# Dense expert weights built in steps of eight tokens instead of four

## The chip, the cores and the metric

The kernel runs on one core of a Trainium2 chip. The metric is the device time of one execution in microseconds; the kernel before took 1877.42 us (median of three runs, 1877.06 to 1878.47). A profile of one execution comes with it. Engines are called by the profile's names: PE (TensorE matmul; PEld is its weight load), DVE (VectorE), ACT (ScalarE), POOL (GpSimd) and SP (SyncE, which issues most DMAs).

## The reference

The reference is one layer of a hybrid block on 512 tokens plus 16 meta tokens, 1024 features wide: a gated linear recurrence and a latent attention are mixed, and a mixture of 16,384 tiny experts (PEER) follows. Only the experts touch the change:

```python
q = (xt @ w_q).reshape(BLOCK, PEER_HEADS, PEER_QDIM)
s1 = jnp.einsum('chd,nd->chn', q[..., :half], keys1)
s2 = jnp.einsum('chd,nd->chn', q[..., half:], keys2)
...                                   # the 16 best (expert index idx, score ts) of each of 8 heads
g = jax.nn.softmax(ts, axis=-1)
act = jax.nn.gelu(jnp.einsum('chkd,cd->chk', u[idx], xt))
coef = g * act
return jnp.einsum('chk,chkd->cd', coef, v[idx])
```

So each token chooses 8 x 16 = 128 experts with one weight each.

## The kernel before

The tokens are four chunks of 128. For chunk 0 the rows of u and v are fetched by index. For the other three the kernel multiplies with both whole tables, in 128 blocks of 128 experts, and needs the softmax weights in dense form: an array [expert in block, block, token] that is zero wherever the token did not choose the expert. `scatter` (L843) makes that array for one chunk and writes it to DRAM (`gd`), from where the later loop loads it again (`gt`).

For one token, `scatter` forms two one-hot matrices with the 128 choices on the partitions: `hot`, which marks the expert's place in its block, and `hb`, which marks its block; `wj` is `hb` times the choice's weight. The product of `hot` and `wj` on PE, [expert in block, block], is the token's dense weight. Per step of four tokens:

- DVE compares for `hb` (L868, 512 columns, bf16; the four tokens are the innermost index) and for `hot` (L870, 512 columns, f32).
- ACT scales three of the four tokens' columns of `hb` into `wj` (L875), DVE the fourth (L877). Each reads every fourth bf16 element.
- PE does four 128 x 128 f32 products into one PSUM bank, side by side (L878). The trace shows each product as two matmuls.
- ACT copies the bank to `stg` (L879). `stg` is [block, 32 tokens] per partition, so a token's 128 values, which lie side by side in PSUM, go to places 128 bytes apart in SBUF.

After eight steps (32 tokens) SP writes `stg`, which has one buffer, to `gd` (L881). Four such pieces make a chunk, 96 steps the three chunks. `hb`, `hot` and `wj` have two buffers of four tokens each. The banks come from `mm2`, a ring of three (L453).

The three `scatter` generators are interleaved with two other streams by the share of each that is done: `choose` (L757), which finds the best pairs of the next chunk on DVE, and `first_ahead`, which computes the first expert product (u times x, then gelu) ahead of the main loop: nine, ten and twelve blocks beside the three chunks. Such a block is 24 PE matmuls of 128 x 384 (L181 to L183, tile `a`); its weights `ut_w` are split into two float32r parts, one by ACT (L155), one by DVE (L156), and its result goes through ACT's gelu (L820). A scheduler decides in which order the instructions stand on each engine; only the later loop fixes DVE's order (L976).

After the third chunk come the last two first products and then the main loop (`dense`, L958), which alternates a block of the first product with one of the second (tile `y`). Its operands `vh` and `vl` are in pool `vp`, opened before the scatter phase. The first `y` needs `gt`, and so the last `gd` transfer.

Of the kernel before, what the change touches and what calls it, by code (L numbers as in the profile page):

```python
# [21 lines left out]
NK = 8            # 128-row pieces of D_MODEL  # L22
NM = 16           # meta tokens
# [4 lines left out]
NH = 16           # attention heads  # L28
SCALE = 96.0 ** -0.5
PH = 8            # PEER heads  # L30
TOPK = 16
NS = PH * TOPK    # chosen experts of a token
NCAND = 50        # pairs (a, b) of ranks with (a + 1) * (b + 1) <= 16
NEG = -3.0e38
BIG = 1.0e30
# The pair of rank k (from 0) has (a + 1) * (b + 1) <= k + 1: blocks (a0, na, b0, nb) of pairs, by the
# group of four ranks that they can first have.
# [5 lines left out]
CO = (3, 0, 2, 1)    # chunks of queries of a pair of heads: the two sizes of the probabilities in turn  # L43
NJ = 128          # blocks of 128 experts
LAG = 41          # blocks that the first product runs ahead of the second
TS = 32           # tokens of a piece of the dense weights
JG = 4            # blocks of a load of the dense weights
# How the experts of a chunk are computed. Chunk 0: rows of both tables fetched by index.
# Chunks 1 to 3: products with both whole tables, times the dense softmax weights.
NDC = 3  # L50
ORD = (mybir.EngineType.DVE,)
SCA = 3           # tokens of four that ScalarE scales
LT = 2            # blocks of the first product between the two phases
GE = 6            # steps by which the fetches of rows end early
GA = ((0, 2), (2, 5))          # gate tiles that are computed between those of the recurrent branch
# [3 lines left out]
DT = NDC * P      # tokens of the dense chunks  # L59

# columns of the packed per-feature vectors
# [7 lines left out]
class in_order:  # L69
    """Keeps the instructions of the given engines that are traced within in the order of the program."""  # L70
# [22 lines left out]
def now(gen):  # L93
    """Runs a generator through; what it returns."""
    while True:
        try:
            next(gen)
        except StopIteration as e:
            return e.value
# [7 lines left out]
def interleave(*gens):  # L107
    """Runs generators in step, by the share of each that is done."""
    items = [[g, n, 0] for g, n in gens if n]
    while items:  # L110
        it = min(items, key=lambda i: i[2] / i[1])
        try:
            it[2] += next(it[0]) or 1
        except StopIteration:
            items.remove(it)
# [3 lines left out]
def hybrid_block_kernel(ctx: ExitStack, tc, hT, x, win, wkr, vecs, wgate, wrnn, watt, wuq, wukv, wout,  # L119
# [38 lines left out]
    wn = [0, 0, None]         # pieces, more buffers of the parts and their pool  # L158

    def wload(src, n, name):  # L160
        """A weight tile of n columns: its two float32r parts, in pieces of 512 columns."""
# [28 lines left out]
    # K' of a head: 64 rows without position, then the rotated rows twice  # L190
# [12 lines left out]
    def bcast_rms(sq, pieces, dim, dst, name):  # L203
        """dst = sqrt(mean of squares + eps) of every token (column), on all partitions."""
        for t0, n in pieces:
            o = mm1(f"{name}_ss{t0}")
            for k, q in enumerate(sq):
                TE.matmul(o[:, :n], onesP, q[:, t0:t0 + n], start=k == 0, stop=k == len(sq) - 1)
            A.activation(dst[:, t0:t0 + n], o[:, :n], AF.Sqrt, bias=eps_t, scale=1.0 / dim)

    # The projections take h * g; their outcomes are scaled by the token's 1/rms.
# [6 lines left out]
    def proj_tile(wi, full, name, src=None, m=P, w=None):  # L218
        """One tile of w_in: PSUM pieces (first token, tokens, psum); full: with the meta tokens."""
# [22 lines left out]
    def two(tags, name):  # L242
        """Eight [P, T] pieces in the space of two tiles."""
# [56 lines left out]
    def latent_norms():  # L300
        """The rotated key rows of all buffers, the normed latent of keys and values, the queries' scales."""
# [17 lines left out]
    # 8 * log_sigmoid(lambda) = 8 * (min(l, 0) - log1p(exp(-|l|)));  # L319
    # log1p(z) = 2 * atanh(y), y = z / (2 + z) <= 1/3  # L320
# [11 lines left out]
    for d in (13, 11, 9, 7, 5, 3, 1):  # L332
# [8 lines left out]
          for k in range(NK)]                              # recurrent output  # L341
    def sig_tile(wi, name):
        """Sigmoid of a tile of w_in."""
# [10 lines left out]
    def out_rnn(m):  # L354
        """A tile of the recurrent branch's gated outcome."""
# [11 lines left out]
    for hb in range(NK // HB):  # L367
# [53 lines left out]
        # 1 - a^2 = -tanh(log a) * (1 + a^2)  # L421
# [39 lines left out]
    def fm_pieces(pl, name):  # L461
        """A feature-major operand: the two parts of each 128-feature piece."""
# [5 lines left out]
    # the meta tokens in one product: rows hi, hi, lo of the values by hi, lo, hi of the probabilities  # L468
# [8 lines left out]
    def att_pair(pr):  # L477
        """Keys and values of a pair of heads."""
# [19 lines left out]
        # values of the tokens of each chunk  # L498
# [9 lines left out]
    def att_query(pr, j, pair):  # L508
        """Queries of a head."""
# [9 lines left out]
    def att_scores(st):  # L519
# [7 lines left out]
        for (k0, n), sp in zip(pieces, sps):  # L527
            d0 = nk - P - k0         # the diagonal block
# [20 lines left out]
    def att_turn(st):  # L549
        """Probabilities with the keys on the partitions, in parts; those of both heads side by side."""  # L550
# [21 lines left out]
    def att_out(st):  # L572
        """[feature of the pair, query of each head]: a head's own half of the features counts."""
# [54 lines left out]
    xdp = pool(ctx, "xd", "right")  # L628
    mx_ = pool(mixx, "mix")
    # normed input of the experts, feature-major: the dense chunks, then chunk 0  # L630
# [32 lines left out]
    def dense_products(j, o, w=None):  # L663
        """x . u of expert block j for the dense chunks: [expert, token]."""
# [7 lines left out]
    def mixing():  # L672
        """Attention output, gated sum of the branches, residual, second norm."""
# [50 lines left out]
    def key_scores():  # L724
        """Scores of the expert keys, the 16 best of each half."""
# [31 lines left out]
    def choose(i, c):  # L757
        """The 16 best pairs of each head, their indices and softmax weights."""
# [64 lines left out]
    def first_dense(j, o, w=None):  # L823
        """gelu(x . u) of expert block j for the dense chunks: [expert, token]."""
# [18 lines left out]
    def scatter(gi, val, ef):  # L843
        """Dense [expert in block, block, token] weights of a chunk, to DRAM: one-hot products of each token."""
# [17 lines left out]
        for q in range(P // TS):  # L862
            stg = sp_.tile([P, NJ, TS], F32, tag="stg", bufs=1, name=f"stg{gi}_{q}")
            for t4 in range(0, TS, 4):
                o = mm2(f"sc{gi}_{q}_{t4}")
                t0 = q * TS + t4
                hb = sp_.tile([P, P, 4], BF16, tag="hb", bufs=2, name=f"hb{gi}_{t0}")
                V.tensor_tensor(hb, iota4, blk[:, t0:t0 + 4].unsqueeze(1).to_broadcast([P, P, 4]), op=OP.is_equal)  # L868
                hot = sp_.tile([P, 4, P], F32, tag="hot", bufs=2, name=f"hot{gi}_{t0}")
                V.tensor_tensor(hot, iota.unsqueeze(1).to_broadcast([P, 4, P]),  # L870
                                it[:, t0:t0 + 4].unsqueeze(2).to_broadcast([P, 4, P]), op=OP.is_equal)
                wj = sp_.tile([P, 4, P], F32, tag="wj", bufs=2, name=f"wj{gi}_{t0}")
                for u in range(4):
                    if u < SCA:
                        A.activation(wj[:, u, :], hb[:, :, u], AF.Copy, scale=gt_[:, t0 + u:t0 + u + 1])  # L875
                    else:
                        V.tensor_scalar(wj[:, u, :], hb[:, :, u], gt_[:, t0 + u:t0 + u + 1], None, op0=OP.mult)  # L877
                    TE.matmul(o[:, u * P:(u + 1) * P], hot[:, u, :], wj[:, u, :], start=True, stop=True)  # L878
                A.copy(stg[:, :, t4:t4 + 4].rearrange("p j t -> p t j"), o.rearrange("p (t j) -> p t j", t=4))  # L879
                yield  # L880
            nc.sync.dma_start(gd[gi, q], stg)  # L881
# [24 lines left out]
    def first_by_index(c):  # L906
        """coef = softmax weight * gelu(u[idx] . x) of the chosen experts."""
# [31 lines left out]
    def stage(j):  # L939
        """Operands of step j: the parts of u of block j + LAG, of v and of the coefficients of block j."""  # L940
# [61 lines left out]
def _consts():  # L1002
    """Constants that depend on the shapes alone."""
# [22 lines left out]
def _layout(i):  # L1026
# [7 lines left out]
    def tiles(w):                      # [K, N] -> [N / 128][128 of K][K / 128 * 128 of N]  # L1034
# [17 lines left out]
    uq = np.concatenate([uq, uq[..., 80:96], uq[..., 64:80]], -1)               # 3, p, h, 128  # L1052
    uq = uq.reshape(3, P, 8, 2, P).transpose(2, 1, 3, 0, 4).reshape(8, P, 768)
    kv = f["w_ukv"][0].reshape(2, P, 8, 2, 2, 64)                               # k, p, pair, j, (key, value), 64
# [28 lines left out]
```

## Time and profile before

| what | value |
|---|---|
| median of three runs | 1877.42 us |
| lowest, highest | 1877.06, 1878.47 us |
| span of the profiled execution | 1876.3 us |
| PE, DVE, ACT busy over the span | 97%, 78%, 52% |
| mean granted TensorE clock | 0.996 |

The span runs from the first to the last instruction of one profiled execution; the page gives no other time for it. The span lies 1.1 us under the median of the timed runs. The scatter phase, in which the change lies, is the stretch from 720 to 967 us. Busy shares over the whole span mix stages with different limits, so the stage's own rows are what counts.

### The profile page before, as it was taken

To read this page: it belongs to the slowest core of one execution; us is meant where nothing else is said; L and a number is where in the kernel's file an instruction comes from. 1 tells how busy PE (TensorE), PEld (TensorE's weight loads), DVE (VectorE), ACT (ScalarE), POOL (GpSimd) and SP (SyncE) were. 2 spreads that over 40 slices of the span, in tenths; PEclk is the share of its full clock that TensorE was granted. 3 is DMA by queue.
4 is the path that set the end of the run, shared out by engine and by line. 5 is a ranking of instruction groups with operands and counts; after the bars stand their busy time and mean duration, and the time that the engine had idled before them with its cause. 6 is when DMAs were issued, how large, how long until landed. Compare 5 with 4: busy or idle time off the path is not lost.

```text
span 1876.3 us, 28456 instructions
## 1 busy us (share of the span) xinstructions
PE 1821.0 (97%) x9731; PEld 1600.0 (85%) x9731; DVE 1470.3 (78%) x3280; ACT 981.4 (52%) x1915; POOL 356.4 (19%) x295
## 2 busy tenths in 40 slices
PE   8999999999999999999999999999999999999997
PEld 7888778877788888888899999998999999998886
DVE  7787677777546999898858788787887888887775
ACT  5778576766334337999963333333333333333343
POOL 0100000000100000000014344344444444443310
PEclk9999999999999999999999999999999999999999
DMA  5333212112733223454569999989998899988764
GB/s 162 92 101 104 74 54 66 62 55 85 241 113 129 85 85 130 144 194 158 189 225 348 321 318 340 326 300 322 324 334 313 304 331 321 343 309 280 266 223 152
DMA packets 181602, 390.34 MB, mean 208 GB/s; under 512 B 16593, under 2 KB 68305, under 8 KB 179921
## 3 DMA queue, kind: packets, MB, share of 16 engines
q1 hardware_dynamic: 141632, 245.97, 38.9%
q0 software_dynamic: 39536, 142.00, 21.8%
q8 instruction: 76, 1.25, 0.3%
q14 instruction: 70, 0.57, 0.1%
q10 hardware_dynamic: 288, 0.56, 0.1%
HBM read 353.44 MB, written 34.08 MB: 207 GB/s over the span
## 4 chain that ended last, share of the span: by engine, by line
PE 73%; ACT 10%; DMA 6%; DVE 6%; issue 3%; POOL 0%; DVEq 0%; ACTq 0%; SPq 0%; POOLq 0%
PE y L183 8%; PE y L182 8%; PE y L181 8%; PE a L183 7%; PE a L182 7%; PE a L181 7%; ACT stg L879 4%; PE q L181 2%; PE q L182 2%; PE wgr_ps L228 2%; PE q L183 2%; PE wga_ps L228 2%; PE wgn_ps L228 2%; PE sc L878 2%; ACT wj L875 2%
## 5 line engine op out<-in xcount | busy, mean ns | idle before, releaser
L183 PE MATMUL a<-xdh,ut_l 128*128 128x384 f32 x1024 | 346.3, 338 | 4.3 <-DVE ut_l L156 4.3
L181 PE MATMUL a<-xdh,ut_h 128*128 128x384 f32 x1024 | 348.1, 340 | 0.7 <-ACT act L820 0.5
L182 PE MATMUL a<-xdl,ut_h 128*128 128x384 f32 x1024 | 345.7, 338 | 0.3 <-DVE xdl L156 0.3
L155 ACT CAST ut_h<-ut_w 128x512 fp32r<-128x512 f32 x256 | 159.2, 622 | 330.3 <-DMA ut_w<-in_peer_uT_dram 281.7
L183 PE MATMUL y<-vh,cl 128*128 128x512 f32 x768 | 300.6, 391 | 0.0
L182 PE MATMUL y<-vl,ch 128*128 128x512 f32 x768 | 300.3, 391 | 0.0
L181 PE MATMUL y<-vh,ch 128*128 128x512 f32 x768 | 299.0, 389 | 1.3 <-ACT ch L155 1.3
L902 POOL DMA_INDIRECT u<-in_peer_u_dram,eidx x128 | 162.7, 1271 | 682.9 <-DMA gt<-gd 458.5
L902 POOL DMA_INDIRECT v<-in_peer_v_dram,eidx x128 | 175.2, 1369 | 262.6 <-DVE acc L922 233.6
L156 DVE TENSOR_TENSOR ut_l<-ut_w,ut_h 128x512 fp32r<-128x512 f32 x256 | 170.5, 686 | 52.2 <-ACT ut_h L155 51.7
L183 PEld LDWEIGHTS a<-xdh,ut_l 128*128 128x128 f32 x1024 | 193.0, 188 | 5.2 <-DVE ut_l L156 5.0
L181 PEld LDWEIGHTS a<-xdh,ut_h 128*128 128x128 f32 x1024 | 193.0, 188 | 4.7 <-ACT act L820 0.9
L182 PEld LDWEIGHTS a<-xdl,ut_h 128*128 128x128 f32 x1024 | 192.9, 188 | 3.9 <-DVE xdl L156 0.5
L156 DVE TENSOR_TENSOR vl<-vr,vh 128x1024 fp32r<-128x1024 f32 x128 | 157.6, 1232 | 40.6 <-ACT vh L155 40.4
L155 ACT CAST ch<-gt 128x384 fp32r<-128x384 f32 x128 | 65.7, 513 | 233.8 <-DVE gt L952 228.8
L922 DVE SCALAR_TENSOR_TENSOR acc<-v,coef,acc 128x1024 f32<-128x1024 f32 x128 | 164.1, 1282 | 11.3 <-DMA v<-in_peer_v_dram,eidx 9.2
L183 PEld LDWEIGHTS y<-vh,cl 128*128 128x128 f32 x768 | 144.1, 188 | 30.6 <-DVE cl L156 0.3
L181 PEld LDWEIGHTS y<-vh,ch 128*128 128x128 f32 x768 | 144.2, 188 | 30.0 <-ACT ch L155 2.1
L182 PEld LDWEIGHTS y<-vl,ch 128*128 128x128 f32 x768 | 144.1, 188 | 28.4
L913 DVE SCALAR_TENSOR_TENSOR jk<-u,xn 128x1024 bf16<-128x1024 f32 x128 | 156.5, 1222 | 14.7 <-DMA u<-in_peer_u_dram,eidx 12.2
L155 ACT CAST vh<-vr 128x1024 fp32r<-128x1024 f32 x128 | 133.7, 1045 | 31.7 <-PE y L183 26.9
L156 DVE TENSOR_TENSOR cl<-gt,ch 128x384 fp32r<-128x384 f32 x128 | 71.5, 559 | 80.9 <-ACT ch L155 80.9
(349 smaller groups left out, 3569.2 us busy)
## 6 DMA issues: line engine op xcount, KB each, us to landing
ut_w<-in_peer_uT_dram SPq DMA_DIRECT2D x256, 256.0 KB, 6.2
vr<-in_peer_v_dram SPq DMA_DIRECT2D x128, 512.0 KB, 6.4
gd<-stg SPq DMA_DIRECT2D x12, 2048.0 KB, 7.3
gt<-gd SPq DMA_DIRECT2D x96, 256.0 KB, 6.9
wq_w<-in_wq_dram SPq DMA_DIRECT2D x32, 256.0 KB, 2.7
wxr_w<-in_win_dram SPq DMA_DIRECT2D x16, 256.0 KB, 2.7
wgr_w<-in_win_dram SPq DMA_DIRECT2D x16, 256.0 KB, 2.8
wga_w<-in_win_dram SPq DMA_DIRECT2D x16, 256.0 KB, 2.6
```

The lines of the kernel that those rows point to most:

```text
L155: A.copy(dst_hi, src)
L156: V.tensor_sub(dst_lo, src, r32(dst_hi))
L181: TE.matmul(o, lh, rh, start=first, stop=False)
L182: TE.matmul(o, lh, rl, start=False, stop=False)
L183: TE.matmul(o, ll, rh, start=False, stop=last)
L228: TE.matmul(o[:m, :n], lhs, rhs[:, k, t0:t0 + n], start=k == 0 and i == 0, stop=k == NK - 1 and i == 2)
L875: A.activation(wj[:, u, :], hb[:, :, u], AF.Copy, scale=gt_[:, t0 + u:t0 + u + 1])
L878: TE.matmul(o[:, u * P:(u + 1) * P], hot[:, u, :], wj[:, u, :], start=True, stop=True)
L879: A.copy(stg[:, :, t4:t4 + 4].rearrange("p j t -> p t j"), o.rearrange("p (t j) -> p t j", t=4))
L902: G.indirect_dma_start(out=t, out_offset=None, in_=src, in_offset=bass.IndirectOffsetOnAxis(ap=eidx[:, s:s + 1], axis=0))
L913: V.scalar_tensor_tensor(jk, t, 1.0, xn2, op0=OP.mult, op1=OP.mult, accum_out=coef[:, s:s + 1])
L922: V.scalar_tensor_tensor(acc, t, coef[:, s:s + 1], acc, op0=OP.mult, op1=OP.add)
```

## The change

`scatter` works in 16 steps of eight tokens a chunk instead of 32 steps of four.

- `hb` and `hot` of eight tokens are each one DVE instruction of 1024 columns (`hb` as two groups of four tokens, so that the tokens are still the innermost index, by fours).
- All eight columns of `wj` are made on ACT. DVE's `tensor_scalar` is gone.
- `hot` and `wj` no longer have tiles of their own: they take the two buffers each of `vh` and `vl` in pool `vp`.
- The products of a step are recorded one step later, after the next step's one-hots (`products`). Their second bank comes from tag `s`, which has three buffers, besides the ring of three.
- The eviction walks block by block and the four tokens innermost: it writes runs of four values (16 bytes) into `stg` and reads PSUM at steps of 512 bytes.

```diff
-SCA = 3
+SG = 8
...
-                wj = sp_.tile([P, 4, P], F32, tag="wj", bufs=2, name=f"wj{gi}_{t0}")
-                for u in range(4):
-                    if u < SCA:
-                        A.activation(wj[:, u, :], hb[:, :, u], AF.Copy, scale=gt_[:, t0 + u:t0 + u + 1])
-                    else:
-                        V.tensor_scalar(wj[:, u, :], hb[:, :, u], gt_[:, t0 + u:t0 + u + 1], None, op0=OP.mult)
-                    TE.matmul(o[:, u * P:(u + 1) * P], hot[:, u, :], wj[:, u, :], start=True, stop=True)
-                A.copy(stg[:, :, t4:t4 + 4].rearrange("p j t -> p t j"), o.rearrange("p (t j) -> p t j", t=4))
-                yield
-            nc.sync.dma_start(gd[gi, q], stg)
+        def products(t0, hot, wj, stg):
+            q, t8 = divmod(t0, TS)
+            for h in range(0, SG, 4):
+                o = ps.tile([P, 512], F32, tag="s", bufs=3, name=f"sc{gi}_{t0 + h}") if h else mm2(f"sc{gi}_{t0}")
+                for u in range(4):
+                    TE.matmul(o[:, u * P:(u + 1) * P], hot[:, h + u, :], wj[:, h + u, :], start=True, stop=True)
+                A.copy(stg[:, :, t8 + h:t8 + h + 4], o.rearrange("p (t j) -> p j t", t=4))
+            if t8 + SG == TS:
+                nc.sync.dma_start(gd[gi, q], stg)
+        last = None
+        for t0 in range(0, P, SG):
...
+            hb = sp_.tile([P, SG // 4, P, 4], BF16, tag="hb", bufs=2, name=f"hb{gi}_{t0}")
+            V.tensor_tensor(hb, iota4.unsqueeze(1).to_broadcast([P, SG // 4, P, 4]),
+                            blk[:, t0:t0 + SG].rearrange("p (h t) -> p h t", t=4).unsqueeze(2)
+                            .to_broadcast([P, SG // 4, P, 4]), op=OP.is_equal)
+            hot = r32(vp.tile([P, D], F32R, tag="vh", bufs=2, name=f"hot{gi}_{t0}")).rearrange("p (t e) -> p t e", t=SG)
...
+            wj = r32(vp.tile([P, D], F32R, tag="vl", bufs=2, name=f"wj{gi}_{t0}")).rearrange("p (t e) -> p t e", t=SG)
+            for u in range(SG):
+                A.activation(wj[:, u, :], hb[:, u // 4, :, u % 4], AF.Copy, scale=gt_[:, t0 + u:t0 + u + 1])
+            yield
+            if last:
+                products(*last)
+            last = (t0, hot, wj, stg)
+            yield
+        products(*last)
```

Comments and docstrings went as well, so the line numbers shift: the products are L869, the eviction L870, `wj` L888.

What it does to the order on PE shows at the start of the first chunk. Here `a` is a block of the first product, `sc` a bank of the scatter products; before, they stand so:

```order
L182 MATMUL a_7763<-xdl,ut_h_7664 128x384
L878 MATMUL sc_0_0_7702<-wj_0_7707,hot_0_7705 128x128 x4
L183 MATMUL a_7763<-xdh,ut_l_7665 128x384
L878 MATMUL sc_0_4_7717<-wj_4_7722,hot_4_7720 128x128 x2
L181 MATMUL a_7763<-xdh,ut_h_7670 128x384
...
L878 MATMUL sc_0_4_7717<-wj_4_7722,hot_4_7720 128x128 x2
L878 MATMUL sc_0_8_7732<-wj_8_7737,hot_8_7735 128x128 x4
L181 MATMUL a_7763<-xdh,ut_h_7670 128x384
```

In the changed kernel the same place on PE reads:

```order
L183 MATMUL a_7744<-xdh,ut_l_7671 128x384
L869 MATMUL sc_0_7771<-wj_0_7706,hot_0_7704 128x128 x4
L869 MATMUL sc_4_7777<-wj_0_7706,hot_0_7704 128x128 x4
L869 MATMUL sc_8_7796<-wj_8_7719,hot_8_7717 128x128 x4
L869 MATMUL sc_12_7802<-wj_8_7719,hot_8_7717 128x128 x4
L181 MATMUL a_7853<-xdh,ut_h_7734 128x384
```

Products that stood singly or in twos and fours inside a block of the first product now stand, mostly eight or sixteen together, between two blocks.

The second place is ACT at the end of the third chunk, where `stg` is the last piece, `act` a gelu and `vh` a part of the main loop's first operands. Before:

```order
L875 ACTIVATE wj_124_10634<-hb_124_10630,gt_9596 128x128
L155 CAST ut_h_10709<-ut_w_10707 128x512
L820 ACTIVATE act_10612<-a_10587 128x384
L879 COPY stg_3_10437<-sc_3_24_10614 128x4x128
L879 COPY stg_3_10437<-sc_3_28_10629 128x4x128
L155 CAST ut_h_10715<-ut_w_10713 128x512
```

And in the changed kernel:

```order
L888 ACTIVATE wj_120_10371<-hb_120_10367,gt_9436 128x128 x4
L870 COPY stg_3_10204<-sc_112_10380 128x128x4
L870 COPY stg_3_10204<-sc_116_10386 128x128x4
L155 CAST ut_h_10469<-ut_w_10467 128x512
L870 COPY stg_3_10204<-sc_120_10392 128x128x4
L155 CAST vh_10523<-vr_10521 128x1024
L870 COPY stg_3_10204<-sc_124_10398 128x128x4
L155 CAST vh_10546<-vr_10544 128x1024
```

Four evictions instead of two follow the last `wj`, with two other casts between them; the first two casts for `vh` now stand here, since `hot` holds these buffers until then. On PE three whole blocks of the first product follow the last `sc` before the first `y`, in both kernels.

## Rows read from the trace of the kernel before

**Rows 1.** The page, chain that ended last: shares by engine.
```profile
PE 73%; ACT 10%; DMA 6%; DVE 6%; issue 3%; POOL 0%; DVEq 0%; ACTq 0%; SPq 0%; POOLq 0%
```

**Rows 2.** Windows: stretch, length, busy of each engine (instructions), clock, DMA share, GB/s.
```profile
720.00:967.00 247.00, 228.97 (x1501) 212.87 (x1501) 212.76 (x681) 229.81 (x490) 0.00 (x0) 1.00 0.47 166
967.00:1000.00 33.00, 32.17 (x168) 29.52 (x167) 20.21 (x32) 11.10 (x20) 12.05 (x10) 1.00 1.03 363
1000.00:1850.00 850.00, 848.24 (x4188) 758.67 (x4187) 680.42 (x908) 313.21 (x501) 325.89 (x246) 1.00 0.89 308
```

**Rows 3.** Groups, 720 to 967: busy us, mean ns | idle before, its releasers.
```profile
L878 PE MATMUL sc<-wj,hot 128*128 128x128 f32 x768 | 109.6, 285 | 17.8 <-ACT wj L875 12.1 <-DVE hot L870 1.8 <-DVE wj L877 1.3
L879 ACT COPY stg<-sc 128x512 f32<-128x512 f32 x96 | 101.6, 1111 | 4.0 <-DMA gd<-stg 3.0 <-PE sc L878 0.6
L875 ACT ACTIVATE wj<-hb,gt 128x128 f32<-128x128 bf16 x288 | 98.2, 412 | 5.7 <-DVE hb L868 5.2
L878 PEld LDWEIGHTS sc<-wj,hot 128*128 128x128 f32 x768 | 97.8, 191 | 33.6 <-ACT wj L875 31.2 <-ACT stg L879 1.5
L870 DVE TENSOR_TENSOR hot<-iota,it 128x512 f32<-128x512 f32 x96 | 65.7, 684 | 2.7 <-PE sc L878 2.1
...
L868 DVE TENSOR_TENSOR hb<-iota,blk 128x512 bf16<-128x512 bf16 x95 | 39.3, 418 | 14.6 <-ACT wj L875 13.2 <-ACT blk L856 1.4
L155 ACT CAST ut_h<-ut_w 128x512 fp32r<-128x512 f32 x61 | 38.2, 629 | 7.7 <-PE a L182 7.6
L877 DVE TENSOR_SCALAR wj<-hb,gt 128x128 f32<-128x128 bf16 x96 | 26.8, 279 | 0.3 <-ACT gt L860 0.3
L820 ACT ACTIVATE act<-a 128x384 f32<-128x384 f32 x30 | 15.1, 502 | 0.2
```

**Rows 4.** Timeline of ACT, 804 to 813: start, length, instructions merged.
```profile
803.88 1.61 ACT L875 ACTIVATE wj<-hb,gt 128x128 f32<-128x128 bf16 x5
...
806.00 2.94 ACT L879 COPY stg<-sc 128x512 f32<-128x512 f32 x3
808.71 0.65 ACT L155 CAST ut_h<-ut_w 128x512 fp32r<-128x512 f32 x1
```

**Rows 5.** Timeline of PE, 962 to 965.5.
```profile
962.90 0.33 PE L183 MATMUL a<-xdh,ut_l 128*128 128x384 f32 x1
963.08 1.95 PE L878 MATMUL sc<-wj,hot 128*128 128x128 f32 x16
964.78 0.42 PE L181 MATMUL a<-xdh,ut_h 128*128 128x384 f32 x1
```

**Rows 6.** Groups of ACT and DVE, other shapes: busy us, mean ns.
```profile
L747 ACT COPY scs<-sc 128x512 f32<-128x512 f32 x16 | 9.4, 588 | 0.9 <-PE sc L745 0.7
L418 ACT ACTIVATE aa<-rr,cl 128x528 f32<-128x528 f32 x8 | 5.9, 737 | 0.1
L426 ACT ACTIVATE rr<-rr 128x528 f32<-128x528 f32 x8 | 4.9, 640 | 0.0
L810 ACT ACTIVATE gate<-gate 128x128 f32<-128x128 f32 x4 | 1.2, 311 | 0.0
L803 DVE TENSOR_TENSOR work<-sf,cand_pos 128x1600 bf16<-128x1600 bf16 x3 | 3.0, 983 | 0.0
L913 DVE SCALAR_TENSOR_TENSOR jk<-u,xn 128x1024 bf16<-128x1024 f32 x128 | 156.5, 1222 | 14.7 <-DMA u<-in_peer_u_dram,eidx 12.2
```

**Rows 7.** Timelines of ACT, SP and PE at the end of the phase.
```profile
964.17 2.04 ACT L879 COPY stg<-sc 128x512 f32<-128x512 f32 x2
...
966.23 0.33 SPq L881 DMA_DIRECT2D gd<-stg  x1
...
978.63 0.45 PE L181 MATMUL y<-vh,ch 128*128 128x512 f32 x1
```

More of the change, by code (lines that the diff above doesn't have):

```diff
@@ L861, in scatter @@
         yield
[L862 to L871, printed above, removed]
-                wj = sp_.tile([P, 4, P], F32, tag="wj", bufs=2, name=f"wj{gi}_{t0}")
-                for u in range(4):
-                    if u < SCA:
-                        A.activation(wj[:, u, :], hb[:, :, u], AF.Copy, scale=gt_[:, t0 + u:t0 + u + 1])
-                    else:
-                        V.tensor_scalar(wj[:, u, :], hb[:, :, u], gt_[:, t0 + u:t0 + u + 1], None, op0=OP.mult)
-                    TE.matmul(o[:, u * P:(u + 1) * P], hot[:, u, :], wj[:, u, :], start=True, stop=True)
-                A.copy(stg[:, :, t4:t4 + 4].rearrange("p j t -> p t j"), o.rearrange("p (t j) -> p t j", t=4))
-                yield
-            nc.sync.dma_start(gd[gi, q], stg)
@@ new lines, in scatter @@
+        last = None
+        for t0 in range(0, P, SG):
+            if t0 % TS == 0:
+                stg = sp_.tile([P, NJ, TS], F32, tag="stg", bufs=1, name=f"stg{gi}_{t0 // TS}")
+            hb = sp_.tile([P, SG // 4, P, 4], BF16, tag="hb", bufs=2, name=f"hb{gi}_{t0}")
[3 more added lines that the diff above has]
+            hot = r32(vp.tile([P, D], F32R, tag="vh", bufs=2, name=f"hot{gi}_{t0}")).rearrange("p (t e) -> p t e", t=SG)
+            V.tensor_tensor(hot, iota.unsqueeze(1).to_broadcast([P, SG, P]),
+                            it[:, t0:t0 + SG].unsqueeze(2).to_broadcast([P, SG, P]), op=OP.is_equal)
+            wj = r32(vp.tile([P, D], F32R, tag="vl", bufs=2, name=f"wj{gi}_{t0}")).rearrange("p (t e) -> p t e", t=SG)
[6 more added lines that the diff above has]
+            yield
```

## The prediction

> **What bounds the kernel now.** The chain of waits, read first, is three quarters PE, with ACT second at 10% [rows 1]. That is a mean over stages, so the windows come next: before 1000 us and after it the kernel has different limits. From 1000 to 1850 us PE is busy 848.2 of 850 us [rows 2]; that stage is PE's, and a phase that ends earlier before it moves its start by as much. In the scatter phase, 720 to 967 us, all three engines look full: PE 229.0, DVE 212.8, ACT 229.8 of 247 us [rows 2]. Who waits for whom decides. In the groups of that stretch the products of `sc` sat idle 17.8 us on PE and 33.6 us on its weight load, nearly all of it for ACT's `wj`, and DVE's `hb` waited 13.2 us for `wj` too [rows 3]. ACT itself waited 17.2 us (247 less 229.8), in its largest groups 7.7 for PE, 5.2 for `hb`, 4.0 before evictions [rows 3].
>
> PE's 229 us is not its need, since it is counted busy while its pipeline stretches between small groups. Undisturbed, a matmul of 384 columns follows the last after 0.18 us (962.90 to 963.08), and eight products, sixteen matmuls, take 1.70 us (963.08 to 964.78) [rows 5]. 30 blocks (30 gelus in the window [rows 3]) of 24 x 0.18 = 4.3 us are 130 us, and 48 times eight products 82 us: 212 us. So ACT, with 230 us, sets the phase; PE could do it in 212.
>
> **The change part by part.**
>
> *`wj` all on ACT.* 96 more scalings. In a row they cost (1.61 - 0.41) / 4 = 0.30 us each, with 0.41 the length of a single one [rows 3, 4]. Plus 28.8 us on ACT, the bound.
>
> *The eviction in runs.* Now 1.111 us long [rows 3]; in a row each takes (808.71 - 806.00) / 3 = 0.90 us [rows 4]. The same copy of a bank with both sides in order, `scs`, is 0.588 us [rows 6]: writing at steps of 128 bytes costs 0.52 us. The new write puts four values side by side. The read, though, now steps through PSUM by 512 bytes, and no ACT or DVE instruction of this trace does that. Bounds: 0.588 us if the read is free; 1.111 if a stepped read is as slow as a stepped write and the slower side sets the pace; 1.11 + 0.52 = 1.63 if runs of four don't help and both add up. A gain beyond 0.588 I exclude, since that is the copy without any step. What speaks for a cheap step: `wj` reads every fourth bf16 of SBUF and is 412 ns long; a scale taken from a tile costs 737 - 640 = 97 ns (same 528 columns with and without it), which leaves 315 ns, against 311 ns for 128 columns side by side [rows 3, 6]. So a step is not slow as such; the 128-byte step was. I take the low end, 0.588 us, the nearest copy of a PSUM bank. In a row it overlaps its neighbour by 0 to 0.21 us (what the old one does, 1.111 - 0.90); with half of that it takes 0.48. Saved: 96 x (0.90 - 0.48) = 40 us of ACT.
>
> [...]
>
> *DVE.* `hb` of 1024 columns: between 418 ns at 512 and 983 ns at 1600 bf16 columns, with the same four-index form, lies 0.68 us [rows 3, 6]; 48 x 0.68 = 33 for 39. `hot` of 1024: 1.22 us like the f32 operation of `jk` [rows 6]; 48 x 1.22 = 59 for 66. The 96 scalings, 26.8 us, go [rows 3]. Together 40 us less on an engine that was not the bound: no gain in itself. [...]
>
> *Products a step behind.* They no longer wait for a `wj` just begun; PE's idle 17.8 us was not the bound. What gains is ACT: `hb` is ready a step of eight earlier and DVE has slack, so the 5.2 us for `hb` go. The 7.7 and 4.0 us (PE's blocks, `gd`) stay. New is a wait of `wj` for buffers: two steps of eight, both held while sixteen products run (3.4 us). Behind such a `wj` on ACT stand evictions, the casts of the next `ut_h` and a gelu, which PE needs one block later. In the new order two casts and a gelu stand beside each block, some 1.4 us that ACT can do meanwhile. I allow 0 to 5 us.
>
> Phase: ACT 229.8 + 28.8 - 40 = 218.6, plus 11.7 to 16.7 of waits: 230 to 235 us, mid 232.8; minus 14 against 247. PE's 212 lies under it.
>
> *The end of the phase.* After the last eviction (964.17 + 2.04 = 966.21) `gd` goes out at 966.23 and the first `y` starts at 978.63, 12.4 us later, with no time to spare: PE has just done the three blocks between [rows 7]. Now one cast of `ut_h` (0.5 us in a row) and one of `vh` stand before the last eviction; a cast of twice `ut_h`'s 512 columns takes about 1.0 us. Queued behind them: `gd`, `gt`, the first `y`. Some of it would have passed while `sc` ran: plus 0 to 2, I take 1 us. The casts and DVE differences for `vh` and `vl` that moved here from an earlier time stand where ACT is busy 11.1 and DVE 20.2 of 33 us [rows 2]: free. SP issues the same transfers.
>
> Sum: -14 + 1 = -13 us. On the profiled span 1876.3 gives 1863.3; the median of the runs lies 1.1 us above the span, so 1877.4 - 13 = 1864 us.
>
> **Rivals.**
>
> *1. The read by steps costs what the write did (slower).* The eviction stays at 0.90 us in a row, the added `wj` stay: ACT 258.6 + 11.7 to 16.7, phase 270 to 275, plus 24 to 29 and the 1 us at the end: 1902 to 1907, say 1904. It decides as soon as the eviction saves less than 28.8 / 96 = 0.30 us, that is, is longer than 0.81 us. For it: the operand was turned round, not straightened, one side still steps. Against: `wj`'s free steps. In its bad form, 1.63 us, another 50 us: about 1954.
>
> *2. The engines get in each other's way (about no change).* `wj` and the products share two buffers; in some seventeen places of the new order sixteen products stand together. If ACT stood idle 0.8 us at each, with little else to do, 13 us would be lost and the time be 1877. For it: four evictions in a row at the ends of pieces, behind a single `stg`. Against: the casts and gelus queued there, and PE's reserve of 20 us. An eviction between 0.75 and 0.9 us would also end here.
>
> *3. The gain is not passed on.* DMA is 0.89 busy from 1000 us on [rows 2]; if it set that stage, an earlier start would only wait. Against: PE busy 848.2 of 850. This too would be about 1877.
>
> **How the numbers follow.** Forecast 0.60, with 1858 to 1871 as its own range (waits 0 to 5, the end 0 to 2, overlap 0 to 0.21 us an eviction). Rival 1 0.21, its bad form 0.05, rivals 2 and 3 together 0.14. Within 0.2% (3.8 us) is about what a measurement of this kernel can tell from no change. Faster: 0.58 of the forecast and 0.04 of rivals 2 and 3, 0.62. Same: 0.02 and 0.07, 0.09. Slower: 0.26 of rival 1 and 0.03, 0.29. Range 1856 to 1905: below it 0.04, above it the bad form and half of rival 1, 0.15.
>
> **What would show it.** Right: `stg<-sc` about 0.59 us; `wj` x384 at about 0.41; ACT busy about 219 us in a phase of about 233; the products' waits for `wj` mostly gone; the stretch from the first `y` to the end as long as before. Wrong: `stg<-sc` at 1.1 us and ACT near 259 in a phase of 270 (rival 1); short evictions but ACT waiting 30 us for products (rival 2); a phase shorter by 14 us and a later stage longer by as much (rival 3).

## The result and the profile after

The changed kernel takes 1863.88 us (median of four runs, 1858.06 to 1864.84) against 1877.95 us before, 14 us less. The ratio of the two on record is 0.9908, 95% interval 0.9884 to 0.9931; it is not the quotient of these two medians, which is 0.9925 and lies in the interval. By the ratio the gain is 17 us. The prediction was 1864 us. The profiled execution has a span of 1862.3 us, 14.0 us less than before; its own timed run is 1864.08 us.

The windows of the kernel after, the phase cut at its own end (columns as in [rows 2]):

```profile
720.00:948.30 228.30, 219.03 (x1502) 215.38 (x1501) 186.44 (x491) 217.37 (x587) 0.00 (x0) 0.99 0.49 178
...
986.00:1836.00 850.00, 846.42 (x4169) 756.37 (x4168) 677.64 (x903) 313.01 (x498) 325.12 (x246) 1.00 0.89 306
```

ACT, the fourth engine column, is busy 217.4 of 228.3 us, where it was 229.8 of 247 [rows 2]. PE, at 219.0, is now as full as ACT; DVE fell to 186.4. The groups of that window, which answer to [rows 3]:

```profile
L888 ACT ACTIVATE wj<-hb,gt 128x128 f32<-128x128 bf16 x384 | 121.6, 411 | 3.3 <-PE sc L869 1.6 <-DVE hb L879 1.0 <-ACT gt L860 0.8
L869 PE MATMUL sc<-wj,hot 128*128 128x128 f32 x768 | 93.0, 275 | 2.2 <-ACT wj L888 2.0
L869 PEld LDWEIGHTS sc<-wj,hot 128*128 128x128 f32 x768 | 91.6, 192 | 3.1 <-ACT wj L888 2.6 <-ACT stg L870 0.4
...
L884 DVE TENSOR_TENSOR hot<-iota,it 128x1024 f32<-128x1024 f32 x48 | 58.5, 1220 | 8.1 <-PE sc L869 8.0
L870 ACT COPY stg<-sc 128x512 f32<-128x512 f32 x96 | 50.9, 592 | 0.9 <-PE sc L869 0.9
...
L155 ACT CAST ut_h<-ut_w 128x512 fp32r<-128x512 f32 x60 | 36.1, 635 | 2.1 <-PE sc L869 1.5 <-PE a L182 0.5
L879 DVE TENSOR_TENSOR hb<-iota,blk 128x1024 bf16<-128x1024 bf16 x48 | 32.9, 686 | 19.1 <-ACT wj L888 14.3 <-ACT blk L856 4.8
L820 ACT ACTIVATE act<-a 128x384 f32<-128x384 f32 x30 | 14.8, 494 | 4.6 <-PE a L183 4.5
```

The eviction `stg<-sc` is 592 ns, not 1111. `wj` is 411 ns as before, 384 times. The idle of `sc` on PE shrank from 17.8 to 2.2 us (its part for `wj` from 12.1 to 2.0), and on the weight load from 33.6 to 3.1. The end of the phase, in the timelines of ACT, SP and PE (answering to [rows 7]):

```profile
946.24 0.60 ACT L870 COPY stg<-sc 128x512 f32<-128x512 f32 x1
946.71 1.07 ACT L155 CAST vh<-vr 128x1024 fp32r<-128x1024 f32 x1
947.66 0.61 ACT L870 COPY stg<-sc 128x512 f32<-128x512 f32 x1
...
948.29 0.33 SPq L872 DMA_DIRECT2D gd<-stg  x1
...
961.08 0.50 PE L181 MATMUL y<-vh,ch 128*128 128x512 f32 x1 [1.79 <-ACT ch L155]
```

The last eviction ends at 948.27, 17.9 us earlier than before, and the first `y` starts 17.5 us earlier. So 3.5 us of the gain are gone again between the first `y` and the end: that stretch took 1876.3 - 978.6 = 897.7 us before and 1862.3 - 961.1 = 901.2 us after. The chain of waits, three quarters PE before, has only 30% of PE in the kernel after (the shares add up to 62% of the span; the page gives none for the rest):

```profile
PE 30%; issue 16%; POOL 6%; DMA 5%; DVE 4%; ACT 1%; DVEq 0%; POOLq 0%; ACTq 0%
```

At 1686 us PE waits 2.8 us for `ch`; on the chain behind it stand 5.3 us of the transfer `gt<-gd` (from 1678.83 us), and from there it follows transfers and fetches back through the main loop. Whether this belongs to the change is one of the questions below.

### The profile page after: what moved, and what is told of

Its sections match the earlier page's. It is cut to its first block, busy times and chain, and to the rows that moved or that the text cites. A ratio compares the mean times of both kernels' runs of the same rounds, so it can differ in the third digit from the quotient of the medians.

```text
span 1862.3 us, 28323 instructions
## 1 busy us (share of the span) xinstructions
PE 1811.8 (97%) x9731; PEld 1601.3 (86%) x9731; DVE 1444.0 (78%) x3088; ACT 968.5 (52%) x2011; POOL 355.2 (19%) x295
## 4 chain that ended last, share of the span: by engine, by line
PE 30%; issue 16%; POOL 6%; DMA 5%; DVE 4%; ACT 1%; DVEq 0%; POOLq 0%; ACTq 0%
PE y L183 5%; PE y L181 5%; PE y L182 5%; PE a L183 4%; POOL v L915 4%; PE a L181 4%; PE a L182 4%; PE sc L869 4%; DMA v<-in_peer_v_dram,eidx 3%; POOL u L915 2%; DMA u<-in_peer_u_dram,eidx 1%; DVE hot L884 1%; DMA gt<-gd 1%; DMA ut_w<-in_peer_uT_dram 0%; DVE ut_l L156 0%
```

## The experiments

Theory A: ACT's sum sets the phase, and the cheap eviction is what lowered it. Theory B: the larger steps and the products a step behind did it. The kernels ran on several chips, on which the kernel before took 1878 to 1886 us; so ratios to its runs beside them count, and phases are read from profiles, from the cast of the first `blk` to the end of the last eviction: 247.3 us before, 229.0 after.

**The eviction alone.** The kernel before with

```diff
-A.copy(stg[:, :, t4:t4 + 4].rearrange("p j t -> p t j"), o.rearrange("p (t j) -> p t j", t=4))
+A.copy(stg[:, :, t4:t4 + 4], o.rearrange("p (t j) -> p j t", t=4))
```

> The kernel before with one edit: the eviction writes runs of four values and reads PSUM at steps of 512 bytes. Theory A (ScalarE's sum sets the scatter phase, and the eviction is what made it smaller): stg<-sc falls from 1.11 to about 0.59 us, ScalarE's busy time between 720 us and the end of the phase from 230 to about 180 us, TensorE (212 us undisturbed) becomes the bound, the phase shrinks from 247 to 222 to 232 us, and the time is 1853 to 1863 us. Theory B (the gain of the changed kernel comes from steps of eight and products a step behind): the eviction is shorter but the phase stays at 240 us or more, 1870 us or more.

Ratio 0.9864 (0.9837 to 0.9892), against 0.9908 for the whole change; the two intervals just overlap, but the phase, 222.4 us, is 6.6 us shorter than with the whole change, so the one edit is at least as good. Its window and its eviction's group:

```profile
722.50:943.80 221.30, 218.20 (x1494) 210.65 (x1493) 209.17 (x681) 193.75 (x489) 0.00 (x0) 1.00 0.52 184
```

```profile
L879 ACT COPY stg<-sc 128x512 f32<-128x512 f32 x96 | 54.0, 588 | 9.3 <-PE sc L878 6.2 <-DMA gd<-stg 2.7
```

ACT falls by 36 us to 193.8, where 50 us and about 180 were expected, and the phase by 25, no further, because PE is now the one that is always busy (218.2 of 221.3 us), and evictions wait 6.2 us for it. By the ratio the time on the first chip would be 0.9864 x 1877.95 = 1852 us, 1 us below A's range. Theory A holds. B as the main cause is refuted: with small steps and products in the same step the phase is far below B's 240 us.

**The eviction, and all scalings on ACT.** On top of that

```diff
-SCA = 3
+SCA = 4
```

> The kernel before with the eviction in runs and all four scalings of a step on ScalarE; steps stay at four tokens, products in the same step. Theory A: ScalarE's sum is 180 + 96 x 0.32 = 211 us, near TensorE's 212; phase 225 to 235 us, time 1857 to 1868 us, slower than the kernel with the eviction alone by 0 to 8 us. Theory B: 1872 us or more, since the steps are still small and nothing is a step behind.

Ratio 0.9937 (0.9913 to 0.9961), phase 236.7 us.

```profile
717.00:952.50 235.50, 226.63 (x1493) 214.07 (x1492) 196.00 (x585) 220.95 (x585) 0.00 (x0) 0.99 0.48 173
```

The 96 scalings cost ACT 221.0 - 193.8 = 27.2 us and the phase 14: this part of the change is a loss. By the ratio 1866 us, in A's range. The raw 1871.65 us lies just under B's limit, but on a chip where the kernel before took 1885.74. Two sizes were missed: ACT's sum was expected at 211 us, and the loss against the eviction alone at 0 to 8 us, where the raw medians of the same chip are 12 us apart.

**The old eviction in the changed kernel.**

```diff
-A.copy(stg[:, :, t8 + h:t8 + h + 4], o.rearrange("p (t j) -> p j t", t=4))
+A.copy(stg[:, :, t8 + h:t8 + h + 4].rearrange("p j t -> p t j"), o.rearrange("p (t j) -> p t j", t=4))
```

> The changed kernel with the old eviction (writes at steps of 128 bytes, reads PSUM in order). Theory A: stg<-sc is 1.11 us again, ScalarE's sum is 220 + 96 x 0.5 = 268 us, the phase 275 to 285 us, the time 1905 to 1917 us: slower than the kernel before by 28 to 39 us. Theory B: the steps of eight and the step behind keep most of their gain, 1880 us or less.

Ratio 1.0074 (1.0040 to 1.0108): slower than before, as A says and B does not, but by 14 us and not by 28 to 39; phase 261 us. By the ratio that is 1892 us, between the ranges of the two theories.

```profile
720.00:979.50 259.50, 232.97 (x1505) 222.32 (x1505) 186.89 (x489) 255.09 (x587) 0.00 (x0) 0.97 0.44 157
```

ACT is busy 255 of 259.5 us. My 268 had counted 0.5 us an eviction; the two kernels differ by (255.1 - 217.4) / 96 = 0.39. And ACT waits only 4 us, where it waited 17 in the kernel before, so something in the rest of the change does remove waits.

**Products in the same step**, in the changed kernel:

```diff
-            yield
-            if last:
-                products(*last)
-            last = (t0, hot, wj, stg)
-            yield
-        products(*last)
+            products(t0, hot, wj, stg)
+            yield
+            yield
```

> The changed kernel with the products of a step recorded in the same step. Theory A: ScalarE's sum stays at 220 us; TensorE waits for wj, but has room; phase longer by 0 to 6 us, time 1864 to 1870 us. Theory B: the step behind is the gain, and without it the time goes back to 1873 us or more.

```profile
717.50:944.70 227.20, 219.29 (x1493) 213.55 (x1493) 186.87 (x490) 218.60 (x587) 0.00 (x0) 0.99 0.50 179
```

Ratio 0.9921 (0.9894 to 0.9948), phase 228.2 us against 229.0. The step behind gives nothing that shows. Against the kernel with the same eviction and scalings in steps of four (236.7 us) the steps of eight, with their tiles and the second source of banks, give 8 us.

**The same with the old eviction**, to see whether the step behind helps where ACT is the only bound (the edits of the two experiments above together):

> The changed kernel with the old eviction and with the products in the same step, to compare with the old eviction and products a step behind (phase 261 us, ScalarE busy 255 of 260 us, 4 us of waits). Theory F (where ScalarE is the bound, the step behind is what takes its waits away): the waits come back to 10 us or more and the phase is 268 us or longer. Theory G (the larger steps and the six banks take them away, the step behind nothing): the phase is 261 us again, within 2 us, with ScalarE 98% busy.

```profile
718.00:977.80 259.80, 234.10 (x1496) 220.87 (x1495) 188.32 (x489) 255.72 (x587) 0.00 (x0) 0.97 0.44 156
```

Ratio 1.0075 (1.0049 to 1.0101), phase 261 us, ACT 98% busy: G, as far as the step behind goes, which is not what removes ACT's waits. What does was not separated: besides eight tokens an instruction and the second source of PSUM banks, all scalings stand on ACT here, which leaves ACT further behind PE, for whose blocks it waited 7.6 us before and does not wait here, and frees DVE, which makes `hb` (188.3 us busy, 212.8 before). The old eviction with small steps and all scalings on ACT was not run. Only the waits for `hb` can be read from the other runs. With all scalings on ACT, steps of four and the cheap eviction they are nearly gone too:

```profile
ACT wj L875 <- DVE hb L868: 0.8, 2, 0.5
```

With DVE keeping its quarter they stay, in steps of four (6.0 us, the eviction alone) and of eight (7.3 us, the quarter below). So these waits go with DVE's scalings (or with how far ACT is behind), and not with the size of the steps.

**Runs of two**, in the changed kernel:

```diff
-A.copy(stg[:, :, t8 + h:t8 + h + 4], o.rearrange("p (t j) -> p j t", t=4))
+A.copy(stg[:, :, t8 + h:t8 + h + 4].rearrange("p j (a b) -> p a j b", b=2), o.rearrange("p (a b j) -> p a j b", a=2, b=2))
```

> The changed kernel with the eviction in runs of two values (8 bytes) instead of four. If two accesses beside each other are enough for a full-speed write, stg<-sc stays at 0.59 us and the phase as it is. If every jump of 128 bytes costs its share, half of the values jump, stg<-sc is about 0.59 + 0.52 / 2 = 0.85 us and the phase some 15 to 20 us longer. That the step of 512 bytes in the read costs nothing holds in both cases.

```profile
L870 ACT COPY stg<-sc x96: 579/636/694, 726.6 to 948.3; 128x512 f32<-128x512 f32 x96
```

Shortest, median and longest are 579, 636 and 694 ns; in the kernel after the median is 592. So two values side by side take away nearly all of the 0.52 us; the phase is 229.5 us. This version ran once only, so its time is not compared.

**A quarter, and an eighth, of the scalings on DVE**, in the changed kernel (the eighth with `u == 7`):

```diff
+if u % 4 == 3:
+    V.tensor_scalar(wj[:, u, :], hb[:, u // 4, :, u % 4], gt_[:, t0 + u:t0 + u + 1], None, op0=OP.mult)
+else:
     A.activation(wj[:, u, :], hb[:, u // 4, :, u % 4], AF.Copy, scale=gt_[:, t0 + u:t0 + u + 1])
```

> The changed kernel with the fourth of every four scalings back on VectorE. Theory A (ScalarE's sum still sets the phase, at 220 us): ScalarE falls by 96 x 0.32 = 31 us to 190, VectorE rises from 188 to 215, and TensorE's 212 is what is left as the bound; the phase is 3 to 8 us shorter than the changed kernel's, the ratio to the kernel before 0.985 to 0.989. Rival C (VectorE, which makes the low halves of the weights too, is late for TensorE when it is so full): the phase is as long as the changed kernel's or longer, ratio 0.991 or more.

> The changed kernel with one scaling of eight on VectorE: ScalarE about 204 us, VectorE about 195 to 200, TensorE 212 undisturbed. If a second bound at TensorE's 212 to 220 is reached, the phase is 221 us as with a quarter on VectorE, ratio to before 0.986 to 0.989; if ScalarE's sum still counts in part, 224 to 227 us and 0.989 to 0.991.

Quarter: ratio 0.9873 (0.9854 to 0.9892), phase 221.1 us. Eighth: 0.9889 (0.9870 to 0.9908), phase 219.5 us. Their windows, quarter first:

```profile
721.00:942.10 221.10, 216.42 (x1500) 215.38 (x1499) 203.77 (x588) 191.78 (x494) 0.00 (x0) 0.98 0.51 185
```

```profile
716.00:934.90 218.90, 213.25 (x1498) 211.81 (x1497) 194.70 (x539) 203.01 (x539) 0.00 (x0) 1.00 0.52 186
```

ACT differs by 11 us and the phase by 1.6 the other way, so ACT's sum no longer counts: PE is the fullest engine in both, and the phase ends 7 to 9 us above the 212 us estimated as PE's undisturbed need. The granted clock was 0.98 in the quarter's window and 1.00 in the eighth's, so the 1.6 us say nothing of the split itself. Nor is DVE the bound, which is busy 203.8 us in one and 194.7 in the other, and 209.2 with the eviction alone. With the eviction alone these are the fastest versions, 7 to 10 us of phase ahead of the change. The quarter and the changed kernel, timed on the same chip, took 1859.35 and 1863.56 us. The three fastest do not differ beyond their intervals.

**Both kernels once more**, unchanged:

> The kernel before, unchanged, profiled again beside its own timed runs. Theory D (the 3.5 us that the changed kernel lost between its first y and the end come and go from run to run, with the transfers of the main loop): that stretch, 897.7 us in the first profile, lies between 898 and 908 us here. Theory E (the changed kernel's main loop is longer for a reason of its own, its earlier start or its moved casts): it is 898 us again, within 1 us.

> The changed kernel, unchanged, profiled again. Theory D: the stretch from the first y to the end lies anywhere between 898 and 908 us, and the scatter phase is 229 us again, within 1 us. Theory E: it is 901 us again, within 1 us, and above that of the kernel before on this chip.

The changed kernel's ratio came out as 0.9912 (0.9886 to 0.9938). The weight loads of `y` in the two new profiles (before again, after again: first and last start):

```profile
L181 PEld LDWEIGHTS y<-vh,ch x768: 186/188/330, 978.0 to 1870.9; 128*128 128x128 f32 x192
```

```profile
L181 PEld LDWEIGHTS y<-vh,ch x768: 186/188/329, 959.0 to 1850.9; 128*128 128x128 f32 x192
```

From the first `y` to the end of the span (before, after, before again, after again): 897.7, 901.2, 903.0, 902.0 us. The kernel before, run again, has the longest; in the other experiments it lies between 897.5 (old eviction, no step behind) and 908.0. The phase repeats within 1.5 us (247.3 and 248.6; 229.0 and 229.1). Theory D: the lost 3.5 us come and go with the execution (or with the chip, which was not separated). In this second pair the spans are 1881.0 and 1861.0 us: the changed kernel gains 20.0 us, of which 19.5 are the phase. The waits of PE in this stretch, in the first profile before, the first after, and the kernel before run again, show where:

```profile
PE y L181 <- ACT ch L155: 1.3, 2, 0.8
PE y L181 <- ACT ch L155: 5.4, 3, 2.8
PE y L181 <- ACT ch L155: 3.8, 2, 3.0
```

Over all twelve profiles, the two with the shortest stretch (897.5 and 897.7 us) have waits for `ch` of 1.9 and 1.3 us after the first `y`, the ten others (901.2 to 908.0 us) 3.4 to 5.5 us. So the first profile of the kernel before was one of the two short ones. Why PE waits longer for `ch` in ten of the twelve was not tried.

## Why the prediction was right

The mechanism held: ACT was the bound, the cheap eviction relieved it, the added scalings cost part of that back. That the time was met to 0.1 us is luck, for the phase came out 4 us shorter than forecast, and the first pair of executions hid 3.5 us of it. The 14 us between the first medians are the low end of what was measured: the ratio gives 17 us, the second pair of profiles 20, and on that chip the medians (1881.95 and 1863.56 us) are 18 apart, where 13 was forecast.

- *ACT is the bound, PE needs 212 us.* Right. Taking 36 us from ACT shortened the phase by 25, until PE was busy 218 of 221. The 212 stays an estimate from [rows 5]: PE's busy time in the windows ran from 213.3 us (the eighth) to 234.1 (old eviction, no step behind), with 1498 and 1496 recorded matmuls.
- *`wj` all on ACT, plus 28.8 us.* Measured 27.2. (Of the 17.8 us that `sc` sat idle on PE before, 12.1 were for ACT's `wj`, so "nearly all" fits only the weight load, 31.2 of 33.6. Nothing in the sum hangs on it.)
- *The eviction at 0.588 us.* Measured 0.592 (0.588 with steps of four). The in-a-row saving, 0.42 us each and 40 us together, measured 36 to 38 (36 with the one edit, 0.39 each when it was taken back). This was the step on which first place and first rival hung. The rival itself was priced too high: the old eviction in the changed kernel made the phase 14 us longer than before, not 24 to 29, since ACT's sum grew by 25 us and its waits shrank from 17 to 4. Runs of two took 636 ns and runs of four 592, against 1111 ns for single values; ACT's read at steps of 512 bytes shows no cost (592 ns, against 588 for `scs`, which reads in order).
- *DVE.* `hb` 0.686 and `hot` 1.220 us, where 0.68 and 1.22 were forecast. The forecast of no gain missed that it ends ACT's waits for `hb` (next point).
- *Waits of ACT, 11.7 to 16.7 us.* Measured 228.3 - 217.4 = 10.9; with ACT's sum 1.2 us lower this makes the phase 18 instead of 14 us shorter. The waits for `hb` fell from 5.2 to 1.0 us as forecast, but the first reason I gave, products a step behind, was wrong: without the lag they fell too (0.8 us), and in steps of four as well. The second, DVE's slack, fits: they fell wherever DVE no longer scaled. The 7.7 and 4.0 us that were to stay did not: before the casts of `ut_h` 2.1 us are left and before evictions 0.9, while the gelu now waits 4.5 us for PE. The new wait of `wj` for buffers, put at 0 to 5 us, was 1.6. Rival 2, engines in each other's way, did not come.
- *The end of the phase, plus 1 us.* From the last eviction to the first `y` 12.8 us instead of 12.4; PE does wait there now, 1.8 us.
- *The main loop passes the gain on.* In the first pair of profiles 3.5 us were missing, but the kernel before, run again, took 5.3 us longer there too, and the second pair passes all of the gain on; so this is spread between executions, not rival 3.

So in the first pair -18 + 0.4 + 3.5 us make the -14 us for which -14 + 1 stood.

## What to carry to other kernels

When an eviction on ACT has to turn its operand round, try to step through PSUM in the read and write SBUF in runs: here the same copy took 0.59 instead of 1.11 us. Take a change of several parts apart before keeping it: here the eviction's line gave 25 us of the phase, the scalings on ACT took 14 back, the steps of eight with their tiles and banks gave 8, and the step behind nothing. And do not fill the engine that was just relieved beyond the next bound, as long as another engine has the room.

## What the runs showed of the hardware

ACT's copy of a PSUM bank costs the same in order (588 ns) and at steps of 512 bytes (592 ns), while writing single f32 values at steps of 128 bytes to SBUF costs 1111 ns, pairs 636 ns. I had expected the read to be the risk, at a chance of one in four. Also new to me: executions of one kernel on one chip differ by up to 10 us (1878.72 to 1888.33 us for the kernel before, run again), while the scatter phase of each kernel was the same to 1.5 us in its two profiles, so one profile alone does not tell a few microseconds of the main loop.
